# Mixer 0's recurrence with rows (head, token): one kernel change on one Trainium2 core, predicted and tested

## The chip, the core and the metric

The program runs on one core of one Trainium2 chip. The core's engines are called as the profile calls them: PE (TensorE, matmuls; its weight loads are shown apart as PEld), DVE (VectorE), ACT (ScalarE), POOL (GpSimd) and SP (SyncE, which only issues DMAs here). Each engine works through its own queue in order; semaphores tie the queues together. The metric is the time of one execution on the device in microseconds (us); less is better.

## The reference

Two decoder layers over 1024 tokens of width 1024. Only layer 0's mixer is touched. Its first half is an RWKV-7 recurrence with 8 heads of 64 channels:

```python
def step(s, inp):                      # s: heads x 64 x 64, one step for each token
    r_t, w_t, k_t, v_t, a_t, b_t = inp
    sa = jnp.einsum('bhij,bhj->bhi', s, a_t)
    s = s * w_t[:, :, None, :] + sa[..., :, None] * b_t[..., None, :] + v_t[..., :, None] * k_t[..., None, :]
    return s, jnp.einsum('bhij,bhj->bhi', s, r_t)
```

Its result y goes through a group norm over each head's 64 channels, a bonus term and a gate; beside it stands a short gated convolution; both go through `w_out` and are added to the residual. Around it are the input projection `w_in`, an MLP (the FFN), a gated embedding, and layer 1 with an S5 state space mixer. All arithmetic is float32; the big products are made of three products of split halves (`mm3`).

## The kernel before

**The stages of mixer 0.** The tokens are worked in two halves of 512. The eight heads make four pairs; a pair's 2 x 64 channels fill the 128 partitions. So there are eight "pair-halves" n = 0..7 (pair n % 4, token half n // 4). A half's 512 tokens are eight chunks of 64 tokens, and the recurrence is done chunk by chunk in closed form. For a pair-half, five generators run one after another: `rwkv_f` (decays, norms), `rwkv_a` (scaled keys and queries, score matrices, and the triangular inverse of `inverse`), `rwkv_c` (the walk over the eight chunks that carries the state S), `rwkv_g` (group norm, gate) and the two-way `split`.

**What sets the order.** `mixer0_run` steps through eleven stages; a stage runs, say, `g(0)`, `c(1)`, `a(2)` and `f(3)` side by side, one `yield` of each a step, and between the steps it lets a number of units of background work through: matmuls of the input projection (`ps_z`, 512 columns), of the convolution and of the output projection (`ps_wo`). `MIX_STEPS`, `MIX_UNITS` and `MIX_JOBS` are the numbers that set this. The PE's order is exactly the order in which the code issues; the other engines' orders come from a scheduler at build time.

**The names.** In `rwkv_a`, `RA` and `BK` hold for every two chunks r, a, a, r and k, b, b, k (channels on the partitions, tokens in the columns), so that one 128x128 product per head and chunk (`ps_sc`) gives all four 64x64 score blocks, which a mask (`msc`) turns into `SC`. `inverse` builds (I - N)^-1 of a 64x64 triangle for 16 (head, chunk) pairs out of 32x32 products (`ps_ix`, `ps_it`, then `ps_fx`, `ps_ft`) and leaves it in `Rf`. In the last two of these the blocks b = 0 and b = 2 come one after the other, each followed by its copy (`X` on DVE, `Rf` on ACT). `rwkv_t` turns `BK` to tokens on the partitions (`ps_bkt`, `BKt`), two groups of four chunks; `VS` holds v by token for one half of the partitions and sa for the other.

In `rwkv_c` a chunk takes three steps, and the state S is one 128x128 block-diagonal matrix of the two heads (`bd` is the mask that keeps it so):
- p1: `ps_c` = RA x S (L728, 128x128) plus SC x V for each head (L731), copied out by DVE as `rhs` (L733)
- p2: `ps_sa` = Rf x rhs (L738), copied by DVE into `VS` (L739)
- p3: `ps_s` = BKt x VS (L742, 128x128), then DVE adds it to S (L748) and multiplies by the decay `DC` and the mask (L749); PE adds SC x VS to `ps_c` (L752), and ACT copies that to `Y` (L753)

`rwkv_g` turns `Y` back to channels (`ps_yt`, L784), ACT scales it into `gsq` (L786), PE makes the gate (`ps_gt`, L789), and DVE multiplies.

PSUM in this stage: tag "b" has three banks (`ps_c`, `ps_sa`, `ps_s`, the transposes, `ps_gt`), tag "a" two (`ps_sc` and the inverse), and `ps_z`/`ps_wo` three of their own. SBUF pools wait for a buffer's release by tile.

Of the kernel before, what the change touches and what calls it, by code (L numbers as in the profile page):

```python
# [29 lines left out]
MIX_STEPS = [24, 28, 7, 6, 13]  # L30
# [27 lines left out]
class Trunk:  # L58
# [576 lines left out]
    def rwkv_a(self, st, p, cx):  # L635
# [33 lines left out]

        SC = cx["SC"] = []  # L670
        for g in range(2):
            sc = self.rp.tile([P, 2, 2, 2, P], F32, tag="SC", name="SC", bufs=4)
            for h in range(2):
                hs = slice(64 * h, 64 * h + 64)
                ps = self.pc.tile([P, H], F32, tag="a", name="ps_sc")
                for q in range(4):
# [2 lines left out]
                    nc.tensor.matmul(ps[:, q * P:(q + 1) * P], BK[hs, cc, cs], RA[hs, cc, cs], start=True, stop=True)
                nc.vector.tensor_mul(sc[:, :, h], ps.rearrange("p (q a t) -> p q a t", q=2, a=2),  # L680
                                     self.msc.rearrange("p (o a t) -> p o a t", a=2, o=1).broadcast_to([P, 2, 2, P]))
# [9 lines left out]
    def rwkv_t(self, g, cx):

        nc = self.nc
        BK = cx["BK"]
        ps = self.pc.tile([P, H], F32, tag="b", name="ps_bkt")
        for q in range(4):
            c = 4 * g + q
            nc.tensor.transpose(ps[:, q * P:(q + 1) * P], BK[:, c // 2, (c % 2) * P:(c % 2) * P + P], self.ident)
# [1 line left out]
        nc.scalar.copy(t, ps.rearrange("p (c f) -> p c f", f=P))  # L700
        cx.setdefault("BKt", []).append(t)

    def rwkv_c(self, p, cx):

# [1 line left out]
        DC, RA, SC, Rf, v = (cx[n] for n in ("DC", "RA", "SC", "Rf", "v"))
        VS = self.rp.tile([P, 4, 2, P], F32, tag="VS", name="VS", bufs=1)
        ps = self.pc.tile([P, H], F32, tag="b", name="ps_vt")
        for q in range(4):
            nc.tensor.transpose(ps[:, q * P:(q + 1) * P], v[:, q * P:(q + 1) * P], self.ident)  # L710
# [911 lines left out]
```

## Time and profile before

| what | value |
|---|---|
| median of 3 runs | 2822.08 us (2819.73 to 2825.8) |
| the profiled execution | 2808.02 us, of which its span is 2806.2 us |
| busy in the span | PE 2632.6 us (94%), DVE 2006.2 (71%), POOL 1185.9 (42%), ACT 1026.1 (37%) |
| mixer 0 | from the start to 793 us, where the FFN's first matmul starts |
| granted TensorE clock | 0.974, mean over the span |

A row of grouped instructions reads: line, engine, operation, output<-inputs by the program's names, shapes, xcount | busy us, mean ns of one | idle time of the engine just before them <- what ended it. PE shows two records for each float32 matmul (so 128 matmuls of `ps_sa` are x256) and one for each of the 512-column ones in the split format. Records of matmuls overlap, so what a matmul costs PE is read from one start to the next, not from its duration. In the rows of stretches the columns are: stretch, its length, busy time and count of PE, PEld, DVE, ACT and POOL, the granted clock, the DMA share, GB/s.

### The profile page before, as it was taken

Reading aid. Unit: us, or ns where it says so; the run is one execution under the profiler, and the core shown is the slowest. Engines: PE = TensorE matmul, PEld = TensorE weight load, DVE = VectorE, ACT = ScalarE, POOL = GpSimd, SP = SyncE. Lnnn points to the kernel's source line nnn. Section 1 sums busy time; section 2 is a strip of 40 time slices with the busy share of each in tenths; the row PEclk is TensorE's granted clock in tenths of the full one; section 3 lists DMA queues with packets and bytes.
Section 4 is the critical chain, followed back from the end, with each engine's and each line's share of the span. In section 5 each row is a group of like instructions: output and inputs, shape, how many; then the busy total and the mean of one; then the engine's idle time right before and its main releaser. Section 6 shows DMA issues by size and latency. Waiting matters only on the chain.

```text
span 2806.2 us, 44526 instructions
## 1 busy us (share of the span) xinstructions
PE 2632.6 (94%) x16773; PEld 2087.7 (74%) x16773; DVE 2006.2 (71%) x3267; ACT 1026.1 (37%) x1915; POOL 1185.9 (42%) x1771
## 2 busy tenths in 40 slices
PE   7999899988989899999999998899999999999998
PEld 5777677766667677777788786688788888888877
DVE  5666766776689888988777757722477777777864
ACT  4222422232242344545553534522432322332432
POOL 5443333442243387767663504601243433443410
PEclk9999999999999999999999998999999999999999
DMA  4222311321121133333211214411111111111121
GB/s 110 61 59 76 94 54 39 107 69 43 47 69 45 45 92 96 95 89 93 72 60 57 78 52 132 124 53 46 42 53 50 49 53 53 49 49 53 49 75 61
DMA packets 273427, 188.98 MB, mean 67 GB/s; under 512 B 36110, under 2 KB 255356, under 8 KB 273212
## 3 DMA queue, kind: packets, MB, share of 16 engines
q1 hardware_dynamic: 249232, 158.26, 19.3%
q10 hardware_dynamic: 21084, 19.23, 2.6%
q0 software_dynamic: 2896, 8.65, 0.9%
q8 instruction: 132, 2.16, 0.3%
q14 instruction: 83, 0.68, 0.1%
HBM read 156.98 MB, written 29.10 MB: 66 GB/s over the span
## 4 chain that ended last, share of the span: by engine, by line
PE 65%; DVE 16%; POOL 7%; issue 5%; ACT 3%; DMA 3%; SPq 0%; POOLq 0%; ACTq 0%; DVEq 0%
PE ps_dnx L352 9%; PE ps_up L159 6%; PE ps_up L157 6%; PE ps_up L158 6%; PE ps_dny L352 4%; PE ps_z L157 3%; PE ps_z L158 2%; PE ps_z L159 2%; PE ps_gl L157 2%; PE ps_gl L159 2%; PE ps_gl L158 2%; PE ps_dnz L352 2%; PE ps_g L157 2%; PE ps_g L158 2%; PE ps_g L159 2%
## 5 line engine op out<-in xcount | busy, mean ns | idle before, releaser
L157 PE MATMUL ps_up<-prh,uwh 128*128 128x512 f32 x1024 | 406.8, 397 | 3.6 <-ACT uwh L255 3.6
L159 PE MATMUL ps_up<-prh,uwl 128*128 128x512 f32 x1024 | 408.1, 399 | 1.0 <-POOL uwl L258 1.0
L158 PE MATMUL ps_up<-prl,uwh 128*128 128x512 f32 x1024 | 405.6, 396 | 0.0
L258 POOL TENSOR_TENSOR uwl<-uraw,uwh 128x512 fp32r<-128x512 f32 x136 | 183.1, 1346 | 169.3 <-ACT uwh L255 168.5
L146 POOL TENSOR_TENSOR wlo<-wraw,whi 128x1024 fp32r<-128x1024 f32 x66 | 161.7, 2451 | 183.6 <-ACT whi L145 181.5
L157 PEld LDWEIGHTS ps_up<-prh,uwh 128*128 128x128 f32 x1024 | 195.0, 190 | 49.6 <-ACT uwh L255 4.0
L352 PE MATMUL ps_dnx<-hidh,whi 128*128 128x512 f32 x480 | 198.1, 413 | 35.9 <-DVE ha L355 33.2
L159 PEld LDWEIGHTS ps_up<-prh,uwl 128*128 128x128 f32 x1024 | 194.6, 190 | 46.6 <-POOL uwl L258 1.4
L158 PEld LDWEIGHTS ps_up<-prl,uwh 128*128 128x128 f32 x1024 | 194.7, 190 | 45.5
L271 POOL TENSOR_TENSOR draw<-draw 128x128 f32<-128x128 f32 x120 | 64.5, 538 | 380.5 <-DMA draw<-in_l_ffn_down_dram 305.0
L145 ACT CAST whi<-wraw 128x1024 fp32r<-128x1024 f32 x104 | 108.7, 1047 | 268.1 <-PE ps_z L158 153.7
L355 DVE TENSOR_TENSOR h<-h,ps_dnx 128x512 f32<-128x512 f32 x240 | 164.0, 683 | 57.1 <-PE ps_dnx L352 55.9
L196 POOL TENSOR_TENSOR acc<-acc,sq 128x512 f32<-128x512 f32 x70 | 105.0, 1509 | 214.2 <-ACT sq L195 213.4
L352 PE MATMUL ps_dnx<-hidl,whi 128*128 128x512 f32 x480 | 189.2, 394 | 4.9 <-DVE hidl L317 4.9
L157 PE MATMUL ps_z<-prh,whi 128*128 128x512 f32 x416 | 191.8, 461 | 0.6 <-ACT prh L477 0.6
L352 PE MATMUL ps_dnx<-hidh,wlo 128*128 128x512 f32 x480 | 189.1, 394 | 0.0
L317 DVE TENSOR_TENSOR hidl<-r_up,hidh 128x512 fp32r<-128x512 f32 x188 | 157.6, 850 | 31.9 <-ACT r_up L313 24.5
L355 DVE TENSOR_TENSOR ha<-ha,ps_dnx 128x512 f32<-128x512 f32 x240 | 163.3, 680 | 18.2 <-PE ps_dnx L352 18.0
L255 ACT CAST uwh<-uraw 128x512 fp32r<-128x512 f32 x136 | 83.8, 617 | 246.1 <-PE ps_up L158 233.9
L159 PE MATMUL ps_z<-prh,wlo 128*128 128x512 f32 x416 | 169.4, 407 | 1.6 <-POOL wlo L146 1.6
L158 PE MATMUL ps_z<-prl,whi 128*128 128x512 f32 x416 | 169.9, 408 | 0.9 <-DVE prl L478 0.8
L312 ACT ACTIVATE hidh<-r_up 128x512 fp32r<-128x512 f32 x98 | 61.8, 630 | 233.6 <-DVE r_up L309 230.1
(419 smaller groups left out, 6608.8 us busy)
## 6 DMA issues: line engine op xcount, KB each, us to landing
uraw<-in_l_ffn_up_dram SPq DMA_DIRECT2D x128, 256.0 KB
draw<-in_l_ffn_down_dram SPq DMA_DIRECT2D x120, 256.0 KB
wraw<-in_l_w_in_dram SPq DMA_DIRECT2D x52, 512.0 KB
s5w<-s5w SPq DMA_DIRECT2D x32, 384.0 KB
wraw<-in_l_w_out_dram SPq DMA_DIRECT2D x16, 512.0 KB
wraw<-in_l_ple_gate_dram SPq DMA_DIRECT2D x16, 512.0 KB
wraw<-in_l_glu_w_dram SPq DMA_DIRECT2D x16, 512.0 KB
toep<-kt ACTq DMA_DIRECT2D x32, 240.0 KB
```

The source lines that it names most:

```text
L145: nc.scalar.copy(hi[:, :n], raw[:, :n])
L146: self.lo_engine().tensor_sub(lo[:, :n], raw[:, :n], hi[:, :n].bitcast(F32))
L157: nc.tensor.matmul(ps, wh, xh, start=start, stop=False)
L158: nc.tensor.matmul(ps, wh, xl, start=False, stop=False)
L159: nc.tensor.matmul(ps, wl, xh, start=False, stop=stop)
L196: (eng or nc.vector).tensor_add(acc, acc, sq)
L255: A.copy(uw[m][0], raws["u"])
L258: nc.gpsimd.tensor_sub(uw[m][1], raws["u"], uw[m][0].bitcast(F32))
L271: G.tensor_add(raw[:, 4], raw[:, 0], raw[:, 2])
L317: return lambda: eng.tensor_sub(st[nm][1], t, st[nm][0].bitcast(F32))
L352: nc.tensor.matmul(ps, w[:, a], v, start=id(ps) not in begun, stop=n == 2, skip_group_check=True)
L355: V.tensor_add(hv, hv, ps)
```

## The change

The two heads of a pair stand one above the other: rows are (head, token). Every 64x64 product is made for head 0 in partitions 0..63 and for head 1 in partitions 64..127, as two matmuls next to each other (`mm`), both into one bank. The state is 128x64, without the mask. Keys and scaled b's (`KB`) and v are turned to tokens once a pair-half by `by_token` (three times four transposes, each emptied by four ACT copies of 64x256, into `Kt`, `Bt`, `Vt`). The score products are made for b's first, then for k's: four steps instead of two. The inverse's 32x32 products go chunk by chunk with the four quadrants innermost, `ps_fx` and `ps_ft` too, and their copies come after both blocks. The K x V part of the state update goes into `ps_s` in p1 and the b x sa part in p3; ACT makes `SD` = S x decay; one DVE instruction joins them. `rhs` and `SA` are copied by ACT, `Y` by DVE. y has a bank of its own, `ps_y`, begun in p2 and ended in p3. In `rwkv_g`, ACT empties `ps_yt` by four copies and scales in a fifth instruction. `MIX_STEPS` gives `rwkv_a` 26 steps instead of 24.

```diff
-MIX_STEPS = [24, 28, 7, 6, 13]
+MIX_STEPS = [26, 28, 7, 6, 13]
...
-        SC = cx["SC"] = []
-        for g in range(2):
-            sc = self.rp.tile([P, 2, 2, 2, P], F32, tag="SC", name="SC", bufs=4)
-            for h in range(2):
-                hs = slice(64 * h, 64 * h + 64)
+        SC = cx["SC"] = [self.rp.tile([P, 8, P], F32, tag="SC", name="SC", bufs=4) for _ in range(2)]
+        for m in (1, 0):
+            for g in range(2):
                 ps = self.pc.tile([P, H], F32, tag="a", name="ps_sc")
                 for q in range(4):
-                    cc, par = 2 * g + q // 2, q % 2
-                    cs = slice(par * P, par * P + P)
-                    nc.tensor.matmul(ps[:, q * P:(q + 1) * P], BK[hs, cc, cs], RA[hs, cc, cs], start=True, stop=True)
...
+                    for h in range(2):
+                        hs = slice(64 * h, 64 * h + 64)
+                        nc.tensor.matmul(ps[hs, q * P:(q + 1) * P], KB[hs, m, 4 * g + q], RA[hs, 4 * g + q], start=True, stop=True)
...
+                yield
...
+    def by_token(self, src, tag):
...
+        for q in range(4):
+            nc.tensor.transpose(ps[:, q * P:(q + 1) * P], src[:, q * P:(q + 1) * P], self.ident)
+        t = self.rp.tile([P, 8, 64], F32, tag=tag, name=tag, bufs=1)
+        for h in range(2):
+            for c in range(2):
+                nc.scalar.copy(t[64 * h:64 * h + 64, c:8:2], ps[64 * c:64 * c + 64].rearrange("p (q f) -> p q f", f=P)[:, :, 64 * h:64 * h + 64])
+        return t
...
+        def mm(ps, a, b, start, stop):
+            for s in hs:
+                nc.tensor.matmul(ps[s, 0:64], a[s], b[s], start=start, stop=stop, skip_group_check=True)
...
+            pa = bank("ps_c")
+            mm(pa, SK[:, c, 64:128], V[:, c], True, first)
             if not first:
...
+                mm(pa, RA[:, c, 64:128], S, False, True)
+            rhs = small("rhs")
+            nc.scalar.copy(rhs, pa[:, 0:64])
+            pS = bank("ps_s")
+            mm(pS, K[:, c], V[:, c], True, False)
+            if not first:
+                SD = small("SD")
+                nc.scalar.activation(SD, S, AF.Copy, scale=D_c)
             yield
...
+            pb = bank("ps_sa")
+            mm(pb, Rf[:, c], rhs, True, True)
+            SA = small("SA")
+            nc.scalar.copy(SA, pb[:, 0:64])
+            py = bank("ps_y")
+            mm(py, SK[:, c, 0:64], V[:, c], True, False)
+            if not first:
+                mm(py, RA[:, c, 0:64], S, False, False)
             yield
...
+            mm(pS, B[:, c], SA, False, True)
+            mm(py, SB[:, c, 0:64], SA, False, True)
...
             else:
-                nc.vector.tensor_add(Sn, S, ps3[:, :P])
-                nc.vector.scalar_tensor_tensor(Sn, Sn, D_c, self.bd, ALU.mult, ALU.mult)
...
+                nc.vector.scalar_tensor_tensor(Sn, pS[:, 0:64], D_c, SD, ALU.mult, ALU.add)
+            nc.vector.tensor_copy(Y[:, c], py[:, 0:64])
...
-        nc.scalar.activation(y2, ps, AF.Identity, bias=self.c("l0_ln_b", p), scale=self.c("l0_ln_w", p))
+        for h in range(2):
+            for c in range(2):
+                nc.scalar.copy(y2.rearrange("p (c t) -> p c t", t=64)[64 * h:64 * h + 64, c:8:2],
+                               ps[64 * c:64 * c + 64].rearrange("p (q f) -> p q f", f=P)[:, :, 64 * h:64 * h + 64])
+        nc.scalar.activation(y2, y2, AF.Identity, bias=self.c("l0_ln_b", p), scale=self.c("l0_ln_w", p))
...
         for b in (0, 2):
-            q0, q1 = slice(32 * b, 32 * b + 32), slice(32 * b + 32, 32 * b + 64)
-            for cc in range(4):
-                for h in range(2):
-                    nc.tensor.matmul(px[q1, cc, h], nt(b, cc, h, b, 1), Tm[q0, cc, h], start=True, stop=True)
-            nc.vector.tensor_copy(X[q1], px[q1])
...
+        for c in range(8):
+            for b in (0, 2):
+                nc.tensor.matmul(px[quads[b + 1], c], nt(b, c, 1), Tm[quads[b], c], start=True, stop=True)
         for b in (0, 2):
...
+            nc.vector.tensor_copy(X[quads[b + 1]], px[quads[b + 1]])
```

How it moves instructions is seen in three places. The first is PE's queue in a late chunk of the walk (p1, p2, p3, with three `ps_wo` matmuls, one unit, between them). Before:

```order
L728 MATMUL ps_c<-Sn,RA 128x128
L731 MATMUL ps_c<-VS,SC 64x64 x2
L157 MATMUL ps_wo<-ybh,whi 128x512
L158 MATMUL ps_wo<-ybl,whi 128x512
L159 MATMUL ps_wo<-ybh,wlo 128x512
L738 MATMUL ps_sa<-rhs,Rf 64x64 x2
L157 MATMUL ps_wo<-ybh,whi 128x512
L158 MATMUL ps_wo<-ybl,whi 128x512
L159 MATMUL ps_wo<-ybh,wlo 128x512
L742 MATMUL ps_s<-VS,BKt 128x128
L752 MATMUL ps_c<-VS,SC 64x64 x2
```

In PE's queue of the changed kernel the same p1 and p2 stand so:

```order
L702 MATMUL ps_c<-Vt,SC 64x64 x2
L702 MATMUL ps_c<-Sn,RA 64x64 x2
L702 MATMUL ps_s<-Vt,Kt 64x64 x2
L157 MATMUL ps_wo<-ybh,whi 128x512
L158 MATMUL ps_wo<-ybl,whi 128x512
L159 MATMUL ps_wo<-ybh,wlo 128x512
L702 MATMUL ps_sa<-rhs,Rf 64x64 x2
L702 MATMUL ps_y<-Vt,SC 64x64 x2
L702 MATMUL ps_y<-Sn,RA 64x64 x2
```

All products of the walk have one shape now, and p1 and p2 each hold three pairs of them where p1 held three matmuls and p2 two.

The second place is PE's queue where `rwkv_g` of one pair-half meets chunk 0 or 1 of the next. Before:

```order
L159 MATMUL ps_z<-prh,wlo 128x512
L784 MATMUL ps_yt<-ident,Y 128x128 x4
L789 MATMUL ps_gt<-sg,glu_367 128x512
L728 MATMUL ps_c<-Sn,RA 128x128
L731 MATMUL ps_c<-VS,SC 64x64 x2
```

In PE's queue of the changed kernel, at the same place:

```order
L159 MATMUL ps_z<-prh,wlo 128x512
L779 MATMUL ps_yt<-ident,Y 128x128 x4
L788 MATMUL ps_gt<-sg,glu_367 128x512
L702 MATMUL ps_s<-SA,Bt 64x64 x2
L702 MATMUL ps_y<-SA,SC 64x64 x2
```

The turned `Y` and the gate stand next to each other as before, but one step earlier in the walk: ahead of p3 of chunk 0 instead of p1 of chunk 1.

The third place is ACT's queue in the first pair-half's walk, from the copy of the last turned tile to chunk 2. Before:

```order
L145 CAST whi<-wraw 128x1024
L753 COPY Y<-ps_c 64x128
L145 CAST whi<-wraw 128x1024
L554 ACTIVATE cv<-u,cv_356 128x512
L753 COPY Y<-ps_c 64x128
L145 CAST whi<-wraw 128x1024
L797 CAST ybh<-cv 128x512
L753 COPY Y<-ps_c 64x128
```

In ACT's queue of the changed kernel, for the same chunks:

```order
L145 CAST whi<-wraw 128x1024
L725 COPY rhs<-ps_c 128x64
L735 COPY SA<-ps_sa 128x64
L730 ACTIVATE SD<-Sn,DC 128x64
L145 CAST whi<-wraw 128x1024
L725 COPY rhs<-ps_c 128x64
L554 ACTIVATE cv<-u,cv_356 128x512
L735 COPY SA<-ps_sa 128x64
L730 ACTIVATE SD<-Sn,DC 128x64
L145 CAST whi<-wraw 128x1024
L796 CAST ybh<-cv 128x512
L725 COPY rhs<-ps_c 128x64
```

One copy a chunk becomes three instructions, and the weight casts (`whi`), the convolution and the splits stand between them.

More of the change, by code (lines that the diff above doesn't have):

```diff
@@ L703, in rwkv_c @@
     def rwkv_c(self, p, cx):
         nc = self.nc
[L706 to L710, printed above, removed]
[L711 to L713 removed]
+        DC, RA, (SK, SB), Rf, v = (cx[n] for n in ("DC", "RA", "SC", "Rf", "v"))
@@ L714, in rwkv_c, with bank @@
+        hs = [slice(64 * h, 64 * h + 64) for h in range(2)]
+        def mm(ps, a, b, start, stop):
+            for s in hs:
+                nc.tensor.matmul(ps[s, 0:64], a[s], b[s], start=start, stop=stop, skip_group_check=True)
+        def bank(name):
+            return self.pc.tile([P, H], F32, tag="b", name=name)
+        V = self.by_token(v, "Vt")
         yield
-        self.rwkv_t(1, cx)
-        BKt = cx["BKt"]
+        kb = cx["KB"].rearrange("p m c t -> p m (c t)")
+        K = self.by_token(kb[:, 0], "Kt")
@@ L732, in rwkv_c @@
-            rhs = self.rp.tile([P, P], F32, tag="rhs", name="rhs", bufs=2)
-            nc.vector.tensor_copy(rhs[ar], ps[ar])
-            yield
-            ps2 = self.pc.tile([P, H], F32, tag="b", name="ps_sa")
-            for h in range(2):
-                hc = slice(64 * h, 64 * h + 64)
-                nc.tensor.matmul(ps2[ar, hc], Rf[ar, cc, h], rhs[ar, hc], start=True, stop=True)
-            nc.vector.tensor_copy(VS[ar, cc, par], ps2[ar, 0:P])
+                mm(pa, RA[:, c, 64:128], S, False, True)
@@ L740, in rwkv_c @@
+            if not first:
+                mm(py, RA[:, c, 0:64], S, False, False)
             yield
-            ps3 = self.pc.tile([P, H], F32, tag="b", name="ps_s")
-            nc.tensor.matmul(ps3[:, :P], BKt[c // 4][:, c % 4], VS[:, cc, par], start=True, stop=True)
-            Sn = self.rp.tile([P, P], F32, tag="S%d" % p, name="Sn", bufs=1) if first else S
-            D_c = DC[:, c:c + 1]
+            mm(pS, B[:, c], SA, False, True)
+            mm(py, SB[:, c, 0:64], SA, False, True)
@@ L745, in rwkv_c @@
+            Sn = self.rp.tile([P, 64], F32, tag="S%d" % p, name="Sn", bufs=1) if first else S
             if first:
-                nc.vector.scalar_tensor_tensor(Sn, ps3[:, :P], D_c, self.bd, ALU.mult, ALU.mult)
+                nc.vector.tensor_scalar_mul(Sn, pS[:, 0:64], D_c)
             else:
-                nc.vector.tensor_add(Sn, S, ps3[:, :P])
-                nc.vector.scalar_tensor_tensor(Sn, Sn, D_c, self.bd, ALU.mult, ALU.mult)
-            for h in range(2):
-                hc = slice(64 * h, 64 * h + 64)
-                nc.tensor.matmul(ps[rr, hc], sc[:, h, rr], VS[:, cc, par, hc], start=first, stop=True, skip_group_check=True)
@@ L826, in inverse @@
         for lv in range(1, 5):
[L827 to L833 removed]
+            px = pv(self.pc.tile([P, H], F32, tag="a", name="ps_ix"))
+            for c in range(8):
+                for q, s in enumerate(quads):
+                    nc.tensor.matmul(px[s, c], nt(q, c, q % 2), Tm[s, c], start=True, stop=True)
             X = c8("X")
@@ L836, in inverse @@
             yield
-            pst = self.pc.tile([P, H], F32, tag="a", name="ps_it")
-            pt = pst[:, :256].rearrange("p (c h t) -> p c h t", c=4, h=2)
-            for cc in range(4):
-                for h in range(2):
-                    for q in range(4):
-                        qs = slice(32 * q, 32 * q + 32)
-                        nc.tensor.matmul(pt[qs, cc, h], R[qs, cc, h], X[qs, cc, h], start=True, stop=True)
+            pt = pv(self.pc.tile([P, H], F32, tag="a", name="ps_it"))
+            for c in range(8):
+                for s in quads:
+                    nc.tensor.matmul(pt[s, c], R[s, c], X[s, c], start=True, stop=True)
             T2 = c8("T2")
```

130 lines of the change are left out of this document (46 added, 84 removed).

## The prediction

> **What bounds it now.** I read first the busy time by stretch, then the waits of PE, PE's timeline of single chunks, and the grouped instructions. Busy time before and after the end of mixer 0:
>
> ```profile
> 0.00:793.00 793.00, 711.09 (x7914) 545.47 (x7914) 533.39 (x914) 239.64 (x376) 305.73 (x309) 0.95 0.24 70
> 793.00:2807.00 2014.00, 1921.47 (x8859) 1542.28 (x8859) 1472.76 (x2355) 786.49 (x1540) 880.16 (x1462) 0.98 0.23 66
> ```
>
> Only the first 793 us are touched. There PE is busy for 711 us (90%), DVE for 533 (67%), ACT for 240 (30%). PE stands still for 82 us. Its waits in the stretch (who waits, for what: us in total, times, longest), those that the change can reach:
>
> ```profile
> PE ps_sa L738 <- DVE rhs L733: 11.9, 9, 3.1
> PE ps_s L742 <- DVE VS L739: 5.3, 6, 1.6
> PE ps_ix L833 <- DVE Tm L824: 5.0, 5, 2.1
> PE ps_c L728 <- DVE Sn L749: 4.8, 6, 1.3
> PE ps_fx L857 <- DVE X L858: 4.6, 8, 1.0
> PE ps_ft L867 <- ACT Rf L871: 3.6, 8, 0.5
> PE ps_c L728 <- DVE rn L623: 2.8, 2, 2.6
> PE ps_bo L685 <- DVE SC L680: 2.2, 2, 1.9
> ```
>
> Without `ps_fx` and `ps_ft`, which I count with their matmuls, 32.0 us are waits for DVE. A wait costs more than itself: in the stretch after the longest `rhs` wait the granted clock (the third number from the end) is 0.66, where an undisturbed one has 1.00.
>
> ```profile
> 406.00:416.00 10.00, 7.27 (x25) 5.47 (x26) 3.83 (x8) 1.59 (x3) 1.64 (x1) 0.66 0.18 52
> 100.00:148.00 48.00, 45.39 (x412) 35.30 (x412) 27.34 (x48) 11.29 (x18) 20.82 (x20) 1.00 0.23 67
> ```
>
> The mean of 0.95 over 793 us is a loss of about 40 us, half a us for each of the 82 that PE stood still.
>
> So two things count: PE's own time in mixer 0, and waits that stop it. A us off either comes off the end, since the FFN starts when mixer 0 ends.
>
> **PE: the walk over the chunks.** One chunk in the timeline (start, length, what):
>
> ```profile
> 416.07 0.38 PE L728 MATMUL ps_c<-Sn,RA 128*128 128x128 f32 x2
> 416.39 0.44 PE L731 MATMUL ps_c<-VS,SC 64*64 64x64 f32 x4
> 416.76 0.50 PE L157 MATMUL ps_z<-prh,whi 128*128 128x512 f32 x1
> ...
> 418.02 0.40 PE L159 MATMUL ps_z<-prh,wlo 128*128 128x512 f32 x1
> 418.35 0.44 PE L738 MATMUL ps_sa<-rhs,Rf 64*64 64x64 f32 x4
> 418.73 0.50 PE L157 MATMUL ps_z<-prh,whi 128*128 128x512 f32 x1
> 419.06 0.40 PE L158 MATMUL ps_z<-prl,whi 128*128 128x512 f32 x1
> 419.30 0.39 PE L159 MATMUL ps_z<-prh,wlo 128*128 128x512 f32 x1
> 419.52 0.38 PE L742 MATMUL ps_s<-VS,BKt 128*128 128x128 f32 x2
> 419.84 0.45 PE L752 MATMUL ps_c<-VS,SC 128*64 128x64 f32 x4
> 420.21 1.71 PE L679 MATMUL ps_sc<-RA,BK 64*128 64x128 f32 x16
> 421.85 0.50 PE L157 MATMUL ps_z<-prh,whi 128*128 128x512 f32 x1
> ```
>
> From start to start L728 takes 0.32 us, L731 0.37, L738 0.38, L742 0.32, L752 0.37. Ahead of a narrower shape the wide matmul takes 0.33 instead of 0.23 to 0.24 (418.02 and 419.06), and again behind it (418.73): 0.10 each way. Sixteen records of `ps_sc` take 1.64 us, 0.102 each with 128 columns; at 64 columns I take 0.051. Of L731's 0.37, four records are 0.20, and 0.17 is fixed. Before, a chunk costs 1.76 + 0.10 ahead of L738 = 1.86 us (the 0.32s hold their own lead).
>
> After, p1 and p2 hold 12 records each and p3 8, all narrow: 0.17 + 0.10 fixed and 0.051 a record. If the two heads' matmuls, which use different halves of the rows, run side by side, the records count half: 0.58 + 0.58 + 0.47 = 1.63 us. One after the other: 0.88 + 0.88 + 0.68 = 2.44. Do they? The nearest rows:
>
> ```profile
> 436.35 0.75 PE L843 MATMUL ps_it<-X,R 32*32 32x32 f32 x64
> 437.03 0.50 PE L157 MATMUL ps_z<-prh,whi 128*128 128x512 f32 x1
> 455.60 0.69 PE L857 MATMUL ps_fx<-T,SC 32*32 32x32 f32 x16
> 456.80 0.69 PE L857 MATMUL ps_fx<-T,SC 32*32 32x32 f32 x16 [0.51 <-DVE X L858]
> 457.41 0.50 PE L157 MATMUL ps_z<-prh,whi 128*128 128x512 f32 x1
> 458.90 0.69 PE L867 MATMUL ps_ft<-R,X 32*32 32x32 f32 x16
> 460.04 0.69 PE L867 MATMUL ps_ft<-R,X 32*32 32x32 f32 x16 [0.45 <-ACT Rf L871]
> 460.65 0.50 PE L157 MATMUL ps_z<-prh,whi 128*128 128x512 f32 x1
> 465.17 0.69 PE L599 MATMUL ps_w<-tw,lwa 64*128 64x512 f32 x1
> 465.18 0.69 PE L607 MATMUL ps_a<-tw,lwa 64*128 64x512 f32 x1
> ```
>
> Sixteen records of one 32-row group take 0.61 us (456.80 to 457.41); 64 records over four groups, into one bank, take 0.68. And `ps_w` in the lower 64 rows and `ps_a` in the upper ones start 0.01 apart. So side by side: 64 chunks x (1.63 - 1.86) = -15, less a little where the first chunks have fewer pairs: **-14 us**. The other bound is 64 x 0.58 = +37.
>
> [...] The two heads write into one bank here. [...]
>
> **PE: scores and inverse.** `ps_sc` goes from 16 groups of 16 records (1.64 us) to 32 groups that, side by side, take 8 x 0.102 each: 26.1 us against 16 x (1.64 - 0.17) = 23.5. But many now stand next to products of the same shape: by the order, PE leaves the wide shape 13 times less in all, at 0.37 each, -4.8. Sum **-2 us** (serial: 52.2 - 23.5 - 4.8 = +24).
> `ps_fx` takes 1.81 us (455.60 to 457.41) and `ps_ft` 1.75, since the second block waits for the first one's copy and each runs on a single row group. Alternating blocks with the copies behind cost at most what `ps_it` takes for twice the records, 0.68. 8 x (1.81 + 1.75 - 1.36) = **-18 us** (serial: 1.1 each, -10). The transposes stay twelve a pair-half.
> PE in all: **-34 us**; serial +37 + 24 - 10 = +51.
>
> **DVE and ACT.** By groups (busy us, mean ns | idle before):
>
> ```profile
> L749 DVE SCALAR_TENSOR_TENSOR Sn<-Sn,DC,cst 128x128 f32<-128x128 f32 x60 | 43.8, 730 | 1.7
> L739 DVE COPY VS<-ps_sa 64x128 f32<-64x128 f32 x64 | 18.3, 286 | 39.6 <-PE ps_sa L738 39.2
> L748 DVE TENSOR_TENSOR Sn<-Sn,ps_s 128x128 f32<-128x128 f32 x60 | 16.8, 281 | 22.1 <-PE ps_s L742 22.0
> L753 ACT COPY Y<-ps_c 64x128 f32<-64x128 f32 x64 | 16.5, 258 | 163.0 <-PE ps_c L752 136.7 <-PE ps_yt L784 11.7 <-DVE T L845 4.4
> L700 ACT COPY BKt<-ps_bkt 128x512 f32<-128x512 f32 x16 | 9.3, 584 | 14.8 <-PE ps_bkt L698 14.8
> L871 ACT COPY Rf<-ps_ft 32x256 f32<-32x256 f32 x16 | 5.8, 362 | 9.4 <-PE ps_ft L867 9.2
> ```
>
> A chunk has on DVE now two copies of 286 ns, the add of 281 and L749 of 730: 1.58 us. After, one joined update and one copy out of PSUM, which I take at L748's 281 and L739's 286: 0.57. That is 64 x 1.0 = 65 us less of 533. L749 reads two SBUF operands and swings far above L748, which has one in PSUM; the joined update is of L748's kind. `rhs` and `sa` leave DVE for ACT. ACT's three instructions a chunk instead of one, at 258, add 33 us; twelve copies of turned tiles, at L871's 362, replace three at about L700's 584 (4.3 us against 1.75 a pair-half), and `rwkv_g` gets about 2 more: together 33 + 21 + 16 = 70 on 240 us. ACT is then 39% busy: no bound, and the background matmuls between the steps cover its copies as they cover DVE's.
>
> What of the 32.0 us of waits for DVE, with 16 us of clock behind them (half a us each), goes? Bounds: nothing and all 48. More than half (`rhs`, `VS`: 17.2) changes engine, the rest waits for a DVE with an eighth less to do. I take half: **-24 us**.
>
> **New waits.** In p1 and p2, `ps_s` and `ps_y` are opened and stay open till p3, so when `rwkv_g` issues `ps_yt` and `ps_gt` ahead of p3, the three "b" banks leave one for both: `ps_gt` must wait until ACT has emptied `ps_yt` by four copies, 4 x 0.362 = 1.45, with the signals some 1.8 us. Nothing stands between them in PE's queue; p3 and all background matmuls queue behind, and ACT, DVE wait for p3. In seven stages (the eighth has no walk beside it) that is 13 us, with half again for the clock **+19 us**. Bounds: 0, if the wait only moves others that would have come, and 7 x (3 + 1.5) = +31, if casts stand ahead of the copies. Before, `ps_gt` found a bank free: no wait of it is among PE's. Next, `rwkv_a` is two steps longer, so `ps_w` and `ps_a` of `rwkv_f` come right behind `ps_ft`, and `ps_a` waits for two `Rf` copies (0.72 less what `ps_w` covers): +3. In some stages `rhs` of chunk 1 stands on ACT behind the split of `rwkv_g`'s result: +4.
>
> **Sum:** -34 - 24 + 19 + 3 + 4 = -32 us. The profiled execution took 2808.02 us (span 2806.2), 14 below the median of the runs; taken off the median of 2822.08 this is **2790 us**.
>
> **Rivals.**
> 1. [...] 7%.
> 2. *ACT takes DVE's place as what is waited for*: `rhs` and `SA` now stand behind casts of 1 us and instructions that wait for DVE, and the 24 us aren't had, while the rest stands: 2814. For it: ACT's queue as shown; against: 39% busy, and a copy once its bank is ready runs 258 ns. 22%.
> 3. *All waits on DVE go* (-48): 2766; DVE's load speaks for it. 17%.
>
> My forecast has 52%, and 2% are left for other things. It lies at 2775 to 2805 on its own. The range runs from 2758, below rival 3, to 2822, above rival 2, and leaves out rival 1 and the tails. 0.2% (5.6 us) is about what can be told from no change here: faster holds the forecast, rival 3 and some two thirds of rival 2: 0.83; same 0.08; slower is rival 1 and a tail of rival 2: 0.09.
>
> **What would show it.** Right: pairs of `ps_c` and `ps_y` records that take under 0.5 us for twelve; `ps_fx` under 0.7 us; PE's waits on `Sn` near zero; a new wait of `ps_gt` for ACT's `gsq`, seven times, 1.5 to 2 us; mixer 0 ending near 760 us. Wrong: twelve records that take 0.8 us; long waits of `ps_sa` for ACT; or a later FFN start that gives the gain back.

## The result, and the profile after

| | before | changed |
|---|---|---|
| median, first comparison | 2820.9 us (2813.44 to 2825.8, 4 runs) | 2748.9 us (2747.35 to 2759.97, 4 runs), ratio 0.9755, 95% interval 0.9722 to 0.9789 |
| median, second comparison | 2813.23 us (9 runs) | 2759.05 us (4 runs), ratio 0.9801, interval 0.9780 to 0.9821 |
| profiled execution | 2808.02 us | 2759.97 us |
| mixer 0 ends at | 793.2 us | 751.3 us |
| from there to the end of PE's work | 2006.9 us | 2000.2 us |

The change made the kernel faster by 54 to 72 us; forecast were 32, and 2748.9 lies below the range, whose low end was 2758. The sign and most places were right, the size was not. The profiled pair differs by only 48 us: before's was faster than all four timed runs, the changed kernel's was the slowest of its four.

Busy time of the changed kernel by stretch, up to the end of mixer 0 and behind it (columns as before):

```profile
0.00:751.00 751.00, 690.93 (x9170) 505.36 (x9170) 450.65 (x745) 301.13 (x603) 303.03 (x310) 0.96 0.25 75
751.00:2758.00 2007.00, 1917.08 (x8859) 1538.10 (x8859) 1483.28 (x2359) 788.76 (x1543) 892.33 (x1462) 0.99 0.23 66
```

DVE is busy for 451 us instead of 533, ACT for 301 instead of 240. PE works 20 us less and stands still 22 us less. PE's longest waits in mixer 0 now:

```profile
PE ps_gt L788 <- ACT gsq L783: 11.9, 7, 1.9
PE ps_xt L461 <- DMA xraw<-in_x_dram: 10.7, 2, 6.0
...
PE ps_sa L702 <- ACT rhs L725: 3.3, 5, 0.7
...
PE ps_c L702 <- DVE Sn L747: 1.1, 2, 0.8
...
PE ps_s L702 <- ACT SA L735: 0.6, 1, 0.6
```

The forecast wait of the gate is there, seven times, 1.9 us at most. Of the 17.2 us that PE waited for `rhs` and `VS`, 3.9 are left, now as waits for ACT. The timeline of PE around the first gate shows that wait, and then a chunk:

```profile
393.53 0.60 PE L779 MATMUL ps_yt<-ident,Y 128*128 128x128 f32 x4
395.77 1.12 PE L788 MATMUL ps_gt<-sg,glu 128*128 128x512 f32 x2 [1.65 <-ACT gsq L783]
396.83 0.33 PE L702 MATMUL ps_s<-SA,Bt 64*64 64x64 f32 x4
397.00 0.28 PE L702 MATMUL ps_y<-SA,SC 64*64 64x64 f32 x4
397.21 0.50 PE L157 MATMUL ps_z<-prh,whi 128*128 128x512 f32 x1
...
398.80 0.33 PE L702 MATMUL ps_c<-Vt,SC 64*64 64x64 f32 x4
398.96 0.28 PE L702 MATMUL ps_c<-Sn,RA 64*64 64x64 f32 x4
399.08 0.28 PE L702 MATMUL ps_s<-Vt,Kt 64*64 64x64 f32 x4
399.29 0.51 PE L157 MATMUL ps_z<-prh,whi 128*128 128x512 f32 x1
...
400.60 1.04 PE L672 MATMUL ps_sc<-RA,KB 64*64 64x128 f32 x16
401.57 0.50 PE L157 MATMUL ps_z<-prh,whi 128*128 128x512 f32 x1
```

Twelve records of p1 take 0.49 us from 398.80 to 399.29. The two heads run side by side, though both write into one bank; x3 below tests it.

**How mixer 0 is compared below.** Its end moves by some us from one execution to the next, because the half-clock time in it does. So the main figure is "PE at full clock": from PE's first matmul to the FFN's first, its time in matmuls with the part at half clock counted half, plus the time it stood still. Half is a near count: in before, `ps_z`'s matmuls of 512 columns start 0.43 us apart at a granted clock of 0.50 (412.53 to 414.24) and 0.23 apart at 1.00 (417.10 to 418.02). Before has 677.2 + 77.1 = 754.3 us, the changed kernel 663.0 + 55.7 = 718.7. Second profiles of the same two kernels gave 755.4 and 719.4 (runs z1 and y1 below), while their half-clock time went from 78.5 to 64.8 and from 64.9 to 58.0 us. All runs in one table (us). "Order" is the order of DVE, ACT and POOL behind mixer 0, where versions with the same letter have it the same but for two rows at most. "Rest" runs from the FFN's first matmul to the end of PE's work, and "tables" is a part of it: PE's matmul records 1001 to 2500 behind mixer 0, where a good part of layer 1's tables is made; PE does the same work there in every run. The runs stood on several chips, so medians are compared by their ratio to the one beside them.

| run | mixer 0 ends | PE at full clock | half clock | rest | tables | order | median (before beside it) |
|---|---|---|---|---|---|---|---|
| before | 793.2 | 754.3 | 78.5 | 2006.9 | 363.0 | 0 | 2820.9 |
| z1 before again | 789.9 | 755.4 | 64.8 | 2016.2 | 365.1 | 0 | 2814.36 (2813.56) |
| changed | 751.3 | 718.7 | 64.9 | 2000.2 | 353.3 | A | 2748.9 (2820.9) |
| y1 changed again | 750.2 | 719.4 | 58.0 | 2001.2 | 352.9 | A | 2759.05 (2813.23) |
| x1 copies on DVE | 756.2 | 727.6 | 58.0 | 1997.9 | 349.3 | A | 2764.83 (2814.93) |
| x2 two-step update | 756.5 | 728.6 | 54.6 | 2017.6 | 368.6 | B | 2782.54 (2814.93) |
| y5 both | 758.8 | 735.3 | 44.4 | 2001.5 | 350.2 | A | 2769.82 (2817.34) |
| x3 heads apart | 753.1 | 735.5 | 30.7 | 2018.5 | 371.7 | B | 2781.04 (2814.93) |
| z3 old inverse | 778.2 | 736.0 | 85.3 | 2015.8 | 368.7 | B | 2800.11 (2813.56) |
| x4 seven gates in tag a | 731.9 | 710.7 | 37.5 | 2019.5 | 365.5 | C | 2756.76 (2814.93) |
| y2 six gates | 737.0 | 712.4 | 44.4 | 2000.1 | 351.6 | A | 2740.95 (2813.23) |
| y3 six other gates | 733.9 | 714.2 | 34.1 | 2011.9 | 364.9 | B | 2752.66 (2813.23) |
| y4 gates and scores | 729.6 | 711.7 | 30.7 | 2004.2 | 351.3 | A | 2742.0 (2813.23) |
| x5 before, copies on ACT | 787.5 | 753.2 | 64.9 | 2012.2 | 360.5 | D | 2815.02 (2817.34) |
| x6 before, joined update | 783.3 | 754.1 | 58.0 | 2010.3 | 360.0 | E | 2807.62 (2817.34) |
| z4 before, x5 and x6 | 773.8 | 750.9 | 41.0 | 2017.8 | 366.8 | D | 2804.57 (2813.56) |
| x10 z4 and the inverse | 752.2 | 731.2 | 37.5 | 2020.5 | 368.8 | D | 2779.41 (2817.34) |
| z2 x10 again | 758.2 | 728.8 | 58.0 | 2015.2 | 363.0 | D | 2781.72 (2813.56) |

### The profile page after: what moved, and what is told of

Read it like the earlier page. It is cut to its first block, busy times and chain, and to the rows that moved or that the text cites. A ratio compares the mean times of both kernels' runs of the same rounds, so it can differ in the third digit from the quotient of the medians.

```text
span 2758.1 us, 47137 instructions
## 1 busy us (share of the span) xinstructions
PE 2608.0 (95%) x18029; PEld 2043.5 (74%) x18029; DVE 1933.9 (70%) x3103; ACT 1089.9 (40%) x2145; POOL 1195.4 (43%) x1771
## 4 chain that ended last, share of the span: by engine, by line
PE 66%; DVE 15%; POOL 7%; issue 6%; ACT 3%; DMA 2%; SPq 0%; ACTq 0%; POOLq 0%; DVEq 0%
PE ps_dnx L352 9%; PE ps_up L159 6%; PE ps_up L157 6%; PE ps_up L158 6%; PE ps_dny L352 5%; PE ps_z L157 3%; PE ps_z L158 2%; PE ps_z L159 2%; PE ps_gl L157 2%; PE ps_gl L159 2%; PE ps_gl L158 2%; DVE ha L355 2%; PE ps_g L157 2%; PE ps_g L159 2%; PE ps_g L158 2%
## 5 line engine op out<-in xcount | busy, mean ns | idle before, releaser
L317 DVE TENSOR_TENSOR hidl<-r_up,hidh 128x512 fp32r<-128x512 f32 x188 | 151.9, 820 | 21.2 <-ACT r_up L313 16.4
```

Source lines behind the costliest of these rows:

```text
L317: return lambda: eng.tensor_sub(st[nm][1], t, st[nm][0].bitcast(F32))
```

## The experiments

**x1, x2: each relief of DVE undone in the changed kernel.** x1 copies `rhs` and `SA` on DVE:

```diff
-            nc.scalar.copy(rhs, pa[:, 0:64])
+            nc.vector.tensor_copy(rhs, pa[:, 0:64])
...
-            nc.scalar.copy(SA, pb[:, 0:64])
+            nc.vector.tensor_copy(SA, pb[:, 0:64])
```

> The changed kernel, with `rhs` and `SA` copied by DVE again instead of ACT; the joined state update stays. Theory A (the waits of PE for DVE went almost whole, because the two copies left DVE's queue): 128 copies of about 0.29 us return to DVE (+37 us busy in mixer 0), the waits of ps_sa for rhs and of p3 for SA return with 10 to 14 us, with the clock +15 to +21 us on the changed kernel. Theory B (PE's own time gave more than priced): no effect, within 5 us. Theory C (what relieved DVE is the joined update, not where the copies are made): within 5 us, perhaps some us faster, since ACT's queue with its casts stands no longer in the way.

x2 updates the state in two DVE steps, without `SD`:

```diff
-            if not first:
-                SD = small("SD")
-                nc.scalar.activation(SD, S, AF.Copy, scale=D_c)
...
-                nc.vector.scalar_tensor_tensor(Sn, pS[:, 0:64], D_c, SD, ALU.mult, ALU.add)
+                nc.vector.tensor_add(Sn, S, pS[:, 0:64])
+                nc.vector.scalar_tensor_tensor(Sn, Sn, D_c, self.ones, ALU.mult, ALU.mult)
```

> The changed kernel, with the state updated in two DVE steps as before (an add from PSUM, then a multiplication with two SBUF operands, a tile of ones in place of the mask; 64 columns instead of 128) and without ACT's SD. Theory A (the copies' place): the update lies off the chain, since a chunk's p1 comes about 1.8 us behind the last p3, so within 6 us. Theory C (the update): DVE gets 60 more instructions of 0.3 to 0.7 us, waits for Sn return with 4 us and those of rhs and Y queue behind them: +10 to +20 us. Theory B: no effect.

At full clock they cost 8.9 and 9.9 us against 718.7. Theory A had put 15 to 21 us on x1 and next to nothing on x2, theory C nothing on x1 and 10 to 20 on x2; each of the two reliefs counts, and A was too high. B (PE's own time alone, no effect) falls. The ends of mixer 0 moved by 5 us only, as both runs had 7 to 10 us less of half clock. In the program, x1 stands at a ratio of 0.9818 (0.9800 to 0.9836) to before, y1 at 0.9801 (0.9780 to 0.9821): intervals that overlap. x2 is at 0.9876 (0.9858 to 0.9894), but it has another order behind mixer 0, and its tables alone took 15 us longer. One of x1's waits of PE; then two of x2's, and its update as a group:

```profile
PE ps_sa L702 <- DVE rhs L725: 7.1, 5, 2.0
```

```profile
PE ps_c L704 <- DVE Sn L747: 8.0, 11, 1.9
...
PE ps_sa L704 <- ACT rhs L727: 3.1, 3, 1.7
```

```profile
L747 DVE SCALAR_TENSOR_TENSOR Sn<-Sn,DC,ones 128x64 f32<-128x64 f32 x60 | 31.7, 529 | 0.1
...
L746 DVE TENSOR_TENSOR Sn<-Sn,ps_s 128x64 f32<-128x64 f32 x60 | 12.8, 213 | 24.4 <-PE ps_s L704 24.3
```

The median of the first row's instruction is 277 ns, its mean 529: some are held up (13 of 60 take over 0.4 us), and PE waits for `Sn` behind them.

**y5: both undone.** The two edits together.

> The changed kernel with both undone: `rhs` and `SA` copied by DVE, and the state updated in two DVE steps without ACT's SD; the order behind mixer 0 is that of the changed kernel, row for row. Each alone moved the end of mixer 0 by 5 us (751 to 756). Theory F (two reliefs of one queue, each of which almost suffices): together they cost more than their sum, 15 to 25 us, mixer 0 ends at 766 to 776, with waits for rhs, Sn and SA of 20 us and more. Rival (the two are independent): 10 us, mixer 0 ends near 761; then most of the waits that went were removed by something else, such as the shorter walk on PE or turned keys and values.

16.6 us at full clock. That lies in theory F's range, but it is about the sum of x1 and x2 (18.8), so the two add up and F's mechanism ("more than their sum") falls here. Of the 16.6, 12.7 are time in which PE stands still. The waits are back in both places:

```profile
PE ps_c L704 <- DVE Sn L747: 8.0, 11, 1.9
PE ps_rs L225 <- DVE rs L219: 7.6, 3, 4.1
PE ps_sa L704 <- DVE rhs L727: 7.3, 5, 2.1
```

The end of mixer 0 moved by only 7.5, since this execution had 20 us less of half clock.

**x5, x6, z4, x10, z2: the same reliefs in the kernel before.** x5 moves the copies:

```diff
-            nc.vector.tensor_copy(rhs[ar], ps[ar])
+            nc.scalar.copy(rhs[ar], ps[ar])
...
-            nc.vector.tensor_copy(VS[ar, cc, par], ps2[ar, 0:P])
+            nc.scalar.copy(VS[ar, cc, par], ps2[ar, 0:P])
...
-            nc.scalar.copy(Y[rr, cc], ps[rr])
+            nc.vector.tensor_copy(Y[rr, cc], ps[rr])
```

> The kernel before, with the copies of `rhs` and of sa into VS made by ACT and that of `Y` by DVE, nothing else. Theory F: the waits for rhs and VS (17.2 us) go but for some 4, with the clock 13 to 18 us, mixer 0 ends at 775 to 780 instead of 793. Rival (the copies' engine is not it): DVE's slow update of 730 ns keeps the state late, within 5 us.

x6 joins the update, head by head (`SD` is made by ACT, as S x decay):

```diff
-                nc.vector.tensor_add(Sn, S, ps3[:, :P])
-                nc.vector.scalar_tensor_tensor(Sn, Sn, D_c, self.bd, ALU.mult, ALU.mult)
...
+                    nc.scalar.activation(SD[hc], S[hc, hc], AF.Copy, scale=D_c[hc])
...
+                    nc.vector.scalar_tensor_tensor(Sn[hc, hc], ps3[hc, hc], D_c[hc], SD[hc], ALU.mult, ALU.add)
```

> The kernel before, with the state update in one kind of DVE step that has ps_s as an operand (one for each head's 64x64 block, beside ACT's SD, two small activations), copies left on DVE. Theory F: DVE's 730 ns of L749 become two instructions of 0.2 to 0.28 us instead of add and update, 27 us of DVE go and with them its longest stalls: waits for Sn, rhs and rn of 19.5 us fall by half or more, mixer 0 ends at 776 to 783. Rival: the waits for rhs are set by the queue of big elementwise steps, not by the update; within 5 us.

z4 has both:

> The kernel before with the copies on ACT and the joined update, without the inverse. Each alone left PE's work and gaps at full clock as they were (754 us before, 753 and 754). Theory F (two reliefs of one queue that need each other): together 10 to 17 us, 737 to 744, as undoing both in the changed kernel cost 17. Rival (in the kernel before other waits take their place, on Sn, Tm and the splits): within 4 us of 754, and the relief is worth something only with the rows, where p1 and p2 hold more work for PE beside the chain.

x10 adds the inverse of the change (blocks b = 0 and 2 alternating, copies behind), and z2 is x10 once more:

> The kernel before, with everything that the change does and that needs no rows of (head, token): copies on ACT, joined update, and the alternated last products of the inverse (ps_fx, ps_ft). The walk keeps its 128x128 products, the state its 128 columns, rwkv_g its free bank. Theory F and the prices: inverse -18, waits on DVE -25 with their clock, so mixer 0 ends near 748 to 753, as early as with the whole change: the rows' own gain on the walk (-16 us of PE) is taken back by ps_sc (+5), ps_w (+7) and ps_gt (+12 and its clock). Rival (the rows bring the gain): 770 or later.

> The kernel before with copies on ACT, joined update and alternated inverse, for a second profile. In the first, mixer 0 ended at 752 with 38 us of half clock, against 58 and 65 in the changed kernel. If that low clock time is chance: 58 to 65 us again and an end at 762 to 766, so that the rows are worth some 12 us in mixer 0. If it belongs to the kernel: 752 again, and the rows are worth nothing beside the rest.

Alone they did next to nothing at full clock, -1.1 and -0.2 us; together -3.4. Theory F had 10 to 18 us for x5, x6 and z4 each, and fell; z4's rival ("within 4 us") holds. In x5 the waits moved instead of going; its waits of PE:

```profile
PE ps_c L728 <- DVE Sn L749: 7.8, 8, 1.5
PE ps_ix L833 <- DVE Tm L824: 7.2, 5, 2.1
...
PE ps_sa L738 <- ACT rhs L733: 2.0, 4, 0.8
```

`rhs` fell from 11.9 to 2.0, but `Sn` rose from 4.8 to 7.8 and `Tm` from 5.0 to 7.2. In x6 `Sn` fell to 1.7 and `rhs` rose to 16.8. With the inverse (x10, z2) PE at full clock is at 731.2 and 728.8: the inverse brings 21 there, the whole -24. The early end at 752 in x10, with 37.5 us of half clock, was chance of the clock; z2, the same kernel, had 58.0 and ended at 758. So what else belongs to the change (the rows of (head, token), keys and values turned once, K x V early, the longer `rwkv_a`) is worth about 11 us of PE at full clock beside these three. In the program x10 is at 0.9871 (0.9846 to 0.9896) and z2 at 0.9886, the change at 0.9801 and 0.9755; the difference is more than 11 us, since their tables in the FFN take 10 to 15 us longer (below). Why the two reliefs bring 17 us in the changed kernel and 3 in the kernel before is not shown: no run has the rows alone, or the inverse alone in the kernel before.

**z3: the inverse undone in the changed kernel.** `ps_fx` and `ps_ft` block by block, each followed by its copy:

```diff
-        for c in range(8):
-            for b in (0, 2):
+        for b in (0, 2):
+            for c in range(8):
                 nc.tensor.matmul(px[quads[b + 1], c], nt(b, c, 1), Tm[quads[b], c], start=True, stop=True)
-        for b in (0, 2):
             nc.vector.tensor_copy(X[quads[b + 1]], px[quads[b + 1]])
...
```

> The changed kernel with the last two products of the inverse (ps_fx, ps_ft) block by block again, each block followed by its copy. The prediction's price is 18 us, 10 of PE's work and 8 of waits for X and Rf: PE's work and gaps at full clock rise by 18, mixer 0 ends at 766 to 772. The order behind mixer 0 is the other one, whose rest took 2012 to 2018 us instead of 2000: 2755 + 18 + 15 = 2788 in all. Rival (some of it is slack that the walk takes up): 8 to 12 us in mixer 0.

17.3 us at full clock: the forecast 18 hold. `ps_fx` and `ps_ft` take 10.0 us more of PE's work and 10 more of waits, and `ps_a` 3 less. Mixer 0 ended at 778 and the median is 2800, both later than expected, since this profile had more half clock (85.3 us) than any other. The two waits are back in PE's list of z3:

```profile
PE ps_fx L839 <- DVE X L840: 7.1, 8, 1.9
PE ps_ft L846 <- ACT Rf L851: 3.6, 8, 0.5
```

**x3: heads one after the other.** In each step of the walk all of head 0's products, then all of head 1's:

```diff
-        def mm(ps, a, b, start, stop):
+        def mm(*products):
             for s in hs:
-                nc.tensor.matmul(ps[s, 0:64], a[s], b[s], start=start, stop=stop, skip_group_check=True)
+                for ps, a, b, start, stop in products:
+                    nc.tensor.matmul(ps[s, 0:64], a[s], b[s], start=start, stop=stop, skip_group_check=True)
```

> The changed kernel, with the walk's products of one step issued for head 0 first and then for head 1, instead of in pairs; nothing else changes. Theory B and the prediction's price: neighbouring products now share their 64 rows, so they run one after the other: 12 records take about 0.85 us instead of 0.50, 8 records 0.6 instead of 0.38, 64 x 0.9 = up to +55 us, at least +30 if the two heads still overlap where they meet. [...]

16.8 us at full clock, and the walk's products themselves take 18.5 us more. So the order of issue matters, and the pairs of the change do run side by side. But both numbers of the expectation were too high: PE overlaps the two heads even when their products are queued six and six. Its timeline for p1 of the same chunk:

```profile
400.37 0.32 PE L703 MATMUL ps_c<-Vt,SC 64*64 64x64 f32 x2
400.54 0.22 PE L703 MATMUL ps_c<-Sn,RA 64*64 64x64 f32 x1
400.54 0.27 PE L703 MATMUL ps_c<-Vt,SC 64*64 64x64 f32 x1
...
401.03 0.50 PE L157 MATMUL ps_z<-prh,whi 128*128 128x512 f32 x1
```

Twelve records take 0.66 us instead of 0.49; head 1's first product starts with head 0's second one.

**x4: the gate in a bank of its own.** The first new wait of the forecast, taken away:

```diff
-        ps = self.pc.tile([P, H], F32, tag="b", name="ps_gt")
+        ps = self.pc.tile([P, H], F32, tag="a", name="ps_gt")
```

> The changed kernel, with ps_gt in a bank of tag a (scores and inverse) instead of tag b, so that it need not wait for ACT's four copies of ps_yt. If the new wait is a cost by itself: its 11.9 us in seven places go, with half again for the clock, -12 to -18 us. Rival: p3 or the background behind it then waits for something else that is late (the tag a bank of the inverse, SA, Y), and 0 to -6 us are had.

The wait went, and mixer 0 ended 19 us earlier; at full clock it is 8, between the two forecasts. The program gained nothing: its ratio of 0.9782 (0.9764 to 0.9801) stands beside 0.9755 to 0.9801 of the change. The rest of the program took 19 us longer, 12 of them in the tables. That was not among the theories. PE's order behind mixer 0 is the same, but the build orders DVE's, ACT's and POOL's instructions there anew for each kernel: where layer 1's tables (the small products of 128x32, L1038 to L1060 in the changed kernel) stand among the FFN's additions. From the changed kernel's order to x4's at least 146 of DVE's 2358 instructions there have to move, to before's at least 174; to x1's none.

**y1, y2, y3: the order behind mixer 0, held and changed.** Since the order depends on small things, versions can be found that change mixer 0 alike and differ in the order, or the reverse:

```diff
+        self.gn = getattr(self, "gn", -1) + 1
-        ps = self.pc.tile([P, H], F32, tag="b", name="ps_gt")
+        ps = self.pc.tile([P, H], F32, tag="a" if self.gn in (0, 1, 2, 3, 4, 5) else "b", name="ps_gt")
```

is y2; y3 has `(0, 1, 2, 3, 5, 6)`; y1 is the changed kernel again.

> The changed kernel once more, with a second profile, to tell what is fixed and what varies from one execution to the next. Theory D (what DVE, ACT and POOL do in the FFN behind mixer 0 stands in an order that is made anew for each kernel, and this order is part of the gain): the rest of the program behind mixer 0 takes about 2000 us again (it took 2007 before), mixer 0 some 745 to 752. Theory A (mixer 0 alone): the rest is as before, near 2007, and mixer 0 ends 10 us earlier than in the first profile, near 740.

> The changed kernel with ps_gt in a bank of tag a in the first six pair-halves only. With all seven moved, mixer 0 ended 19 us earlier but the rest took 19 longer; in this version the order of DVE, ACT and POOL behind mixer 0 is the same as in the changed kernel, row for row. Theory D (the order takes the gain back): the rest takes 2000 us, mixer 0 ends near 735, together 16 us less than the changed kernel. Rival E (an earlier FFN is held up by something with a time of its own, such as a DMA or the clock): the rest takes near 2016 whatever the order, and nothing is won.

> As the run with six gates in the unchanged order, but with another six (all but the fifth and the eighth): mixer 0 is nearly the same, and the order behind it is, row for row, that of the run with the heads apart, whose rest took 2018 us. Theory D: mixer 0 ends near 735, the rest takes 2018, together 18 us slower than the run with the unchanged order. Rival E: both runs are equal within 3 us.

y1's rest took 2001.2 us, y2's 2000.1, y3's 2011.9. In the program y2 is at 0.9741 (0.9715 to 0.9766), y3 at 0.9780 (0.9761 to 0.9798), 12 us apart on one chip where mixer 0 speaks for y3 by 3. Rival E falls with y2, whose FFN starts 14 us earlier than the changed kernel's while the rest takes 2000 us all the same. So the order's effect is shown (theory D), though here smaller than the 18 expected. It sits in the tables: in all six profiles of order A they took 349 to 353 us, in all twelve of other orders 360 to 372, and the rest before and behind them differs by a few us without regard to the order. In a stretch of 400 us with the tables, y2 and then y3:

```profile
1000.00:1400.00 400.00, 383.92 (x1711) 303.04 (x1710) 348.86 (x601) 203.84 (x541) 296.63 (x654) 1.00 0.32 87
```

```profile
1000.00:1400.00 400.00, 377.86 (x1653) 297.52 (x1652) 336.56 (x584) 203.43 (x544) 293.35 (x661) 0.97 0.31 84
```

PE gets 58 matmul records less done in y3: it stands still for 22 us instead of 16, and has 20 us of half clock instead of 3 (a mean clock of 0.97). What `ps_dnx`, the FFN's second product, waited for in the whole program, y2 and then y3:

```profile
  DVE ha L355: 28.0, 29
```

```profile
  DVE ha L355: 35.2, 29
```

**y4: gates and scores.** Six gates in tag a (all but the first and the eighth), and b's and k's score products in one step:

```diff
-MIX_STEPS = [26, 28, 7, 6, 13]
+MIX_STEPS = [24, 28, 7, 6, 13]
...
-                yield
+            yield
...
+        ps = self.pc.tile([P, H], F32, tag="a" if self.gn in (1, 2, 3, 4, 5, 6) else "b", name="ps_gt")
```

> The changed kernel with six gates in a bank of tag a (all but the first and the eighth), and the score products in two steps as before instead of four (24 steps of rwkv_a), so that ps_w and ps_a no longer stand behind ps_ft; the order behind mixer 0 is that of the changed kernel, row for row. By the prices of the trace: ps_sc costs 5 us more than before in four steps, ps_w 6 more and 1 of wait; if these are the steps' fault, mixer 0 ends 6 to 12 us earlier than with the gates alone, near 726, and the rest takes 2000. If ps_sc's price is one of its 512 records and the ps_w and ps_a pair is only out of step with the background, 0 to 3 us.

At full clock 711.7, as y2's 712.4; the program is equal too (0.9739, 0.9719 to 0.9758). That is the second forecast, 0 to 3 us, but not by its reason. PE's work fell by 4.7 us, of which `ps_w` 5.9: it stands beside `ps_a` again. New gaps of 4 us took most of that back. y2 and y4 are the fastest versions, 17 to 18 us below the changed kernel on the same chip.

**z1: the kernel before again.**

> The kernel before once more, for a second profile. If the clock's part of mixer 0 is a property of the kernel, half-clock time is again near 78 us and mixer 0 ends within 3 us of 793. If it varies from one execution to the next, as between the two profiles of the changed kernel (65 and 58 us), it lies anywhere from 55 to 85 us and mixer 0 ends at 783 to 797, with PE's gaps unchanged at 77 us.

The second case: 64.8 us of half clock instead of 78.5, gaps of 78.0. The rest took 2016 us instead of 2007 with the same order, so one profile of a rest is uncertain by several us. Still, all six of order A lie at 1998 to 2004, all twelve of other orders at 2007 to 2021. The tables alone are steadier: 363.0 and 365.1 us in the two profiles of before, 353.3 and 352.9 in those of the changed kernel.

## Why the prediction was wrong in size, by its own steps

- *"Only the first 793 us are touched."* This step failed. The order behind mixer 0 changed with the kernel, and the changed kernel has the best one seen (A): its tables took 353.3 and 352.9 us against 363.0 and 365.1, so -10 and -12 where the prediction had nothing. PE's work is the same there; it stood still for 3 and 7 us less, and 14 us less were at half clock. Over the whole rest, whose half clock moves by more from one execution to the next, it is -7 and -15. No view of the profile before could have priced it; that the build orders the other engines was known.
- *"I take half: -24 us"* of the waits for DVE. This step failed too. The bounds (0 and -48) were right, the choice was not. Apart from the inverse's and the gate's waits, PE's gaps fell from 68.9 to 43.4 us, by 25.5 where half of 32.0 is 16. The copies and the update are shown as the cause of half of that: without them (y5) these gaps are 55.9 us. The other 13 went with the rest of the change, and which part of it took them was not tested. In the kernel before, the copies and the update took away only 5 (z4: 64.0). Rival 3 (all waits go) was nearer, and rival 2 (ACT in DVE's place) fell: 3.9 us for `rhs` and `SA`. The reason given ("the rest waits for a DVE with an eighth less to do") goes by mean times: L749 was counted with 730 ns, but it takes 352 as a rule and up to 2.9 us in 19 of 60 cases (last section), and PE can wait for `Sn` behind such a case.
- *The walk, -14 us*: at full clock its products went from 111.7 to 85.1, and the wide matmuls beside them rose by 10.1 for the changes of shape: -16.5. Right, and side by side as taken: 12 records in 0.49 us, with 0.10 for the wide matmul ahead of them 0.59 where 0.58 was taken. One after the other was counted with 0.88, so rival 1, in which the two heads run so, fell, though both heads' products go into one bank; and the order of issue counts (0.49 us against 0.66 in x3).
- *Scores, -2 us*: +5.1 (26.2 to 31.3); sixteen records took 0.97 us where 0.82 was taken. The 4.8 us for fewer changes of shape, which were to pay for it, cannot be seen apart from the walk's.
- *Inverse, -18 us*: PE's work 20.8 to 10.5, gaps 8.2 to 0.4, together -18.1; z3 17.3. Right. After, its rows are these:

```profile
434.25 0.69 PE L839 MATMUL ps_fx<-T,SC 32*32 32x32 f32 x32
...
437.18 0.24 PE L847 MATMUL ps_ft<-R,X 32*32 32x32 f32 x2
437.64 0.69 PE L847 MATMUL ps_ft<-R,X 32*32 32x32 f32 x30 [0.22 <-DVE X L841]
438.26 1.12 PE L599 MATMUL ps_w<-tw,lwa 64*128 64x512 f32 x2
439.15 1.12 PE L607 MATMUL ps_a<-tw,lwa 64*128 64x512 f32 x2
```

- *`ps_w` and `ps_a`, +3*: +5.9 of work and 1.2 of wait. The wait was right; that they no longer run beside each other (0.89 us apart at 438.26 and 439.15, 0.01 before) was missed.
- *`rhs` behind the split, +4*: not seen. All waits of `ps_sa` for `rhs` together are 3.3 us, none above 0.7.
- *The gate, 13 us and 6 of clock*: 11.9 us, seven times. Right. Without it 8 us were had at full clock and 19 at mixer 0's end.
- *The clock*: the terms held -8 and +6 for it; matmul time at half clock went from 67.7 to 56.0 us, worth -5.9.

In the profiled pair: PE at full clock -35.6, clock -5.9, together -41.5 of the 41.9 by which mixer 0 ended earlier, where -32 was the sum; the rest behind it -6.7. That mixer 0 came so near is in part luck: the scores cost 7 us more than forecast and `ps_w` with `ps_a` 4 more, the waits 9.5 less, the clock, the split and the walk 10 less together. The forecast was then taken off the median of 2822.08, as if profiled executions stood alike to their medians. They did not: before's was 13 below the median of its first comparison, the changed kernel's 11 above. That is the rest of the 72 us, and in the second comparison (54 us) it was gone: the profiled execution of y1 lies at its median. Three executions of the changed kernel in the first comparison lie 11 to 13 us below the profiled one, and their granted clock is 0.982 to 0.984 instead of 0.978; by an estimate, 0.005 of the mean clock over 2750 us is 27 us more or less at half clock, some 13 us of work, which would do it. Why the clock differed is not shown; the half-clock time of one kernel's mixer 0 alone was seen to differ by 20 us (x10 and z2).

## What to carry to other kernels

Price what a change does to the order of everything that the build orders itself, behind the change too: an end of a stage that moved by 19 us left the program where it was. Compare stages over the same instructions, at full clock and with two profiles, since half-clock time of one kernel differed by 7 to 20 us. Price a relief in the kernel in which it will stand: the same two reliefs of DVE brought 3 us in the kernel before, where the wait moved to the next place, and 17 in the changed one.

## What the runs showed of the hardware

**The update with two SBUF operands took 0.35 us as a rule and up to 2.9 beside POOL.** DVE and POOL in the kernel before, at one of L749's long executions:

```profile
715.46 2.56 DVE L749 SCALAR_TENSOR_TENSOR Sn<-Sn,DC,cst 128x128 f32<-128x128 f32 x1
```

```profile
715.48 2.39 POOL L146 TENSOR_TENSOR wlo<-wraw,whi 128x1024 fp32r<-128x1024 f32 x1 [7.02 <-ACT whi L145]
```

It ends 0.15 us after POOL's, though the median of L749 is 352 ns. All 19 of the 60 executions of L749 above 400 ns lie beside POOL instructions, 14 of them wholly and the others but for 0.15 to 0.47 us, and all 19 end 0.15 to 0.16 us behind one of POOL; of the 41 short ones 34 lie beside none. In x2 the same form behaves so again (13 of 13 long ones), with 2.48 us at most. The update with `ps_s` as an operand took 232 to 286 ns in all 60, though 8 of these lie wholly beside POOL instructions. What holds L749 up is not shown.

**Half clock came in whole stretches of 3.41 us, as a rule behind waits of PE of 1.2 to 6.2 us.** In the changed kernel each half-clock stretch but the last, which the end cuts off, is 3.41 us or a multiple of it; all 18 begin behind 3.41 us in which PE was busy for at most 65%, with a wait of 1.2 to 6.2 us. That is no threshold: on the same grid of 3.41 us, seven windows of this profile with 48 to 53% were followed by full clock, and in the kernel before 4 of 29 stretches begin behind 70 to 95%. Two of the 18, with the stretch ahead:

```profile
540.12:543.53 3.41, 1.96 (x17) 0.99 (x15) 3.41 (x2) 3.29 (x9) 3.41 (x2) 1.00 0.29 80
543.53:553.77 10.24, 8.01 (x34) 5.09 (x35) 6.30 (x5) 5.98 (x13) 7.28 (x7) 0.50 0.34 110
707.37:710.78 3.41, 1.87 (x18) 1.08 (x16) 3.05 (x4) 1.59 (x4) 2.36 (x1) 1.00 0.01 2
710.78:717.61 6.83, 6.68 (x31) 4.38 (x31) 1.80 (x5) 0.56 (x2) 0.00 (x0) 0.50 0.28 80
```

In the first row PE had waited 1.4 us for `Kt`, in the third it waited for `ybl`, 1.7 us in all; what followed were 10 and 7 us at half clock, and nothing followed behind the seven windows of 48 to 53%. So one us of waiting had no fixed price in clock here, and half a us for each us, as the prediction took it, is a mean at best.
